# Which tiles lead each block's products, and which queue carries the weight sums, in a hybrid mLSTM, attention and conv-FFN layer

## The chip, the cores and the metric

The kernel runs on one core of a Trainium2 chip. The metric is the device time of one execution in microseconds; less is better. Five engines work side by side, each in the order of its own instruction stream: TensorE (PE, with its weight loads as PEld), VectorE (DVE), ScalarE (ACT), GpSimd (POOL) and SyncE (SP). SP, POOL and others can issue DMA transfers, and a transfer is issued when its engine comes to it and its semaphores allow it.

## The reference

One layer on a prompt of 2048 tokens and on 8 sample streams of 16 tokens (128 rows), all fp32, with D = 1024:

```python
qm, km, vm, om, ip, fp, qa, ka, va = split_in(x @ w_in)     # 4 x 512, 2 x 4, 512, 128, 128 columns
...
hm, C1, n1, m1 = mlstm_chunkwise(qm, km, vm, logi, logf, C0, n0, m0, mchunk)   # 4 heads x 128, chunks of 64
hm = (og * head_norm(hm, g_mlstm_norm)).reshape(B, T, M_WIDTH)
qa, ka = rope(qa, pos), rope(ka, pos)                       # 8 query heads, 2 key heads x 64
ha = swa_prompt(qa, ka, va, attn_sinks)                     # window of own chunk + 2, one learned sink a head
mix = jnp.concatenate([hm, ha], axis=-1) @ w_out
h = layer_norm(DEEPNORM_ALPHA * x + mix, ln1_g, ln1_b)
u = h @ w_up                                                # 1024 -> 5632
c = b_conv + sum(ext[:, j:j + T] * w_conv[j] for j in range(3))     # causal, over tokens
a, g = jnp.split(c, 2, axis=-1)
f = (jax.nn.silu(g) * a) @ w_down                           # 2816 -> 1024
y = layer_norm(DEEPNORM_ALPHA * h + f, ln2_g, ln2_b)
```

The outputs are y for both inputs and the states: C, n, m of the mLSTM, the last keys and values, and the last rows of u.

## The kernel before

Every fp32 operand of a large product is split into two parts, `hi` (a cast to the matmul's format on ACT, L217) and `lo` (the rest, a subtraction on DVE, L218); a product is three matmuls (hi x hi, hi x lo, lo x hi). The large products also use a scheme of seven block products in place of eight, which needs sums and differences of quarters of the weights and of the inputs.

The program has three stages: I, the input projection (0 to some 630 us), O, the output projection with the first normalization (to some 885 us), and F, the conv-FFN, up (to some 1840 us) and down (to the end).

**Stage I.** The 17 tiles of 128 tokens go in four blocks of four (`IBLOCKS`; the sample tile, index 4, goes with block 0). The input of a block comes as four quads of 512 KB, `xr1` to `xr4` (two halves of the tokens by two halves of the features); `x_load` issues their loads on SP's queue, `x_steps` makes the sums (t1 to t4) and the splits (numbers, and "b12"). The columns of w_in other than gates, keys and values go in five groups g, each as seven products s = 1 to 7 (`i_product`, L704; with the sample's own matmuls, L714, in block 0); `i_after` takes their results out of PSUM (L771 and L777 among them). The 264 columns of gates, attention keys and values are not in the scheme: they are "direct tiles" (`i_direct`, L730), one for each tile of tokens, 24 matmuls each (8 steps of the features by 3); `i_keys` takes the result out (L738, L739), turns the keys and stores them. Their weights are units ("g", e, u), loaded as 264 KB pieces (`next_raw`) and split (`next_split`) through a ring that they share with the products' weights (512 KB a piece).

`i_begin` writes PE's order as the list `items`: ("p", b, g, s) for a product and ("t", b, i, e) for a direct tile whose weights are load number e. In block 0, tiles 2 and 3 come first, then the products with the sample tile among them. Each block but the last ends with its tiles 0 and 1 and the next block's tiles 2 and 3; the last block ends with its tiles 0 and 1.

`i_dense` walks `items`. It is woven with the chains of the blocks that are ready (mLSTM and attention, tile by tile: L1070 to L1350), by a planner's costs: each yields a number of nanoseconds for its PE work. During direct tiles of blocks after the first, `chains.hold` is set. So PE's order is written out; for DVE, ACT, POOL and SP the framework's list scheduler sets the order of instructions when the program is built, and it may place work well ahead of where it is written.

**The weight sums.** The down projection's weights also need sums. `d_sums(k, step)` does one of 11 of them in three steps: step 0 takes two buffers (`txy`, the tags of xr1 and xr3, which are free of inputs by then) and loads two 512 KB rows of w_down (L844, L845), step 1 and 2 do two DVE subtractions each (L850 to L853, 128x512), and step 2 stores both to DRAM (`zt`, L855, L856). Eight of the sums stand in stage I, four in its third and four in its fourth block, three in stage O. All loads and stores are on SP's queue.

**The attention's sinks.** For each tile and key head, POOL copies the sinks into the last columns of the score buffer (`sc`, L1297), ahead of the score matmuls.

**Names that come up below.** L1077 to L1080 (`m_rows`) put a row of the mLSTM's running maxima through DRAM (`zM`, two buffers in turn) on POOL's queue; L1150 to L1159 (`m_norm`) is the head norm: statistics `bst` on DVE, then `mr` on ACT and DVE.

## Time and profile before

| | before |
|---|---|
| three runs | 2312.8, 2321.06 (median), 2321.19 us |
| profiled execution | 2316.15 us, its span 2314.3 us |
| mean granted clock of TensorE | 0.996 |
| PE busy | 2281.9 us (99%) |
| PEld busy | 2094.9 us (91%) |
| DVE busy | 1808.1 us (78%) |
| ACT busy | 1269.0 us (55%) |
| POOL busy | 279.5 us (12%) |
| DMA | 632 MB, mean 273 GB/s |

The span runs from the first to the last instruction of the profiled execution; the rest of its time lies around it. In rows of instructions, `out<-in` gives the program's names, and the bracket at the end of a timeline row is the time that the engine sat idle before it and what ended it. A matmul's own duration includes its way through the array, and the matmuls overlap, so that counts per window give the rate better than single durations. The granted clock is 1.00 at full speed.

### The profile page before, as it was taken

How to read it: one execution, taken by the hardware profiler on the slowest of the kernel's cores; microseconds unless marked ns; L12 is line 12 of the kernel's file. 1: busy time of each engine (PE TensorE's matmuls, PEld its weight loads, DVE VectorE, ACT ScalarE, POOL GpSimd, SP SyncE). 2: the span in 40 equal slices, each digit the busy share in tenths (PEclk: the TensorE clock that was granted, in tenths of full speed). 3: DMA queues.
4: the chain of work that ended last, by engine and by line, in shares of the span. 5: the costliest groups of instructions: out<-in, count | busy, mean ns of one | idle time of the engine just before them, and what ended most of it. 6: DMA issues, size and time to landing. Idle time of an engine off the chain costs nothing.

```text
span 2314.3 us, 39788 instructions
## 1 busy us (share of the span) xinstructions
PE 2281.9 (99%) x14293; PEld 2094.9 (91%) x14293; DVE 1808.1 (78%) x3075; ACT 1269.0 (55%) x2377; POOL 279.5 (12%) x509
## 2 busy tenths in 40 slices
PE   8999999999999999999999999999999999999998
PEld 8999989989877778999999999999999978888876
DVE  8777687787688888998788777678766786895987
ACT  5453466776766655555656555555555544444442
POOL 0001000000011212121002000013111200100200
PEclk9999999999999999999999999999999999999999
DMA  7888999999977757888778889978898776756743
GB/s 276 287 308 297 301 309 336 314 310 342 315 269 240 240 201 270 303 319 311 276 289 274 306 304 311 315 264 287 312 294 261 225 282 208 261 175 215 255 157 108
DMA packets 300166, 632.38 MB, mean 273 GB/s; under 512 B 47869, under 2 KB 141121, under 8 KB 299969
## 3 DMA queue, kind: packets, MB, share of 16 engines
q1 hardware_dynamic: 295296, 616.14, 77.9%
q0 software_dynamic: 3520, 10.56, 1.4%
q10 hardware_dynamic: 1152, 3.15, 0.4%
q8 instruction: 113, 1.85, 0.3%
q14 instruction: 85, 0.69, 0.1%
HBM read 458.11 MB, written 171.64 MB: 272 GB/s over the span
## 4 chain that ended last, share of the span: by engine, by line
PE 76%; DVE 5%; DMA 4%; issue 2%; ACT 1%; SPq 0%; POOL 0%; DVEq 0%; ACTq 0%; POOLq 0%
PE dps L1873 19%; PE fup L1873 19%; PE dps L704 7%; PE dps L2083 6%; PE fht L2083 6%; PE fup L2083 6%; PE dps L222 2%; PE dps L224 2%; PE dps L223 2%; PE ppo L1348 1%; PE psc L1303 1%; PE ppt L1342 1%; DVE w L218 1%; PE fht L1697 1%; DMA txy<-wdn 0%
## 5 line engine op out<-in xcount | busy, mean ns | idle before, releaser
L1873 PE MATMUL dps<-hh,uw 128*128 128x384 f32 (+1 forms) x1848 | 478.7, 328 | 2.0 <-DVE u L1904 2.0
L1873 PE MATMUL fup<-hh,uw 128*128 128x384 f32 (+1 forms) x1848 | 478.2, 328 | 1.5 <-ACT ua L1894 1.5
L1873 PEld LDWEIGHTS dps<-hh,uw 128*128 128x128 f32 x1848 | 330.5, 188 | 2.2 <-DVE u L1904 2.2
L1873 PEld LDWEIGHTS fup<-hh,uw 128*128 128x128 f32 x1848 | 330.0, 188 | 2.0 <-ACT ua L1894 1.9
L1930 DVE SCALAR_TENSOR_TENSOR cc<-u,cw,cc 128x768 f32<-128x768 f32 (+1 forms) x264 | 258.1, 978 | 64.9 <-ACT cc L1928 55.5
L1873 PE MATMUL fup<-hl,uw 128*128 128x384 f32 (+1 forms) x924 | 302.5, 327 | 1.7 <-DVE hl L218 1.7
L1873 PE MATMUL dps<-hl,uw 128*128 128x384 f32 (+1 forms) x924 | 302.8, 328 | 0.0
L704 PE MATMUL dps<-w,oh 128*128 128x256 f32 x1344 | 254.3, 284 | 0.7 <-DVE zev L777 0.7
L217 ACT CAST uw<-wraw 128x1024 fp32r<-128x1024 f32 x126 | 123.0, 979 | 223.8 <-PE dps L2083 120.1
L218 DVE TENSOR_TENSOR w<-wraw,w 128x1024 fp32r<-128x1024 f32 (+2 forms) x167 | 189.4, 1141 | 56.1 <-ACT w L217 48.9
L217 ACT CAST w<-wraw 128x1024 fp32r<-128x1024 f32 (+2 forms) x167 | 163.0, 985 | 107.3 <-PE dps L704 38.9
L704 PEld LDWEIGHTS dps<-w,oh 128*128 128x128 f32 x1344 | 210.5, 188 | 11.8 <-issue 8.1
L218 DVE TENSOR_TENSOR uw<-wraw,uw 128x1024 fp32r<-128x1024 f32 x126 | 142.4, 1131 | 65.7 <-ACT uw L217 65.5
L704 PE MATMUL dps<-w,ol 128*128 128x256 f32 x672 | 187.8, 279 | 0.0
L704 PE MATMUL dps<-oh,w 128*128 128x256 f32 x896 | 170.9, 285 | 6.6 <-ACT mr L1153 3.8
L1873 PEld LDWEIGHTS fup<-hl,uw 128*128 128x128 f32 x924 | 173.5, 188 | 2.4 <-DVE hl L218 2.3
L2083 PE MATMUL fup<-uw,fu 128*128 128x512 f32 x726 | 174.2, 396 | 0.6 <-DVE uw L218 0.6
L1873 PEld LDWEIGHTS dps<-hl,uw 128*128 128x128 f32 x924 | 173.8, 188 | 0.0
L2083 PEld LDWEIGHTS fup<-uw,fu 128*128 128x128 f32 x726 | 136.6, 188 | 34.1 <-DVE uw L218 1.1
L2083 PE MATMUL dps<-uw,fu 128*128 128x512 f32 x660 | 165.3, 396 | 1.1 <-DVE uw L218 1.1
L1928 ACT ACTIVATE cc<-u,cw 128x768 f32<-128x768 f32 (+1 forms) x132 | 132.2, 1002 | 57.8 <-DVE u L1910 28.5
L704 PEld LDWEIGHTS dps<-oh,w 128*128 128x128 f32 x896 | 142.2, 191 | 13.1 <-ACT mr L1153 4.1
(318 smaller groups left out, 4567.0 us busy)
## 6 DMA issues: line engine op xcount, KB each, us to landing
uw<-zw SPq DMA_DIRECT2D x176, 512.0 KB, 5.1
zw<-uw SPq DMA_DIRECT2D x88, 512.0 KB, 3.7
w<-zws SPq DMA_DIRECT2D x72, 512.0 KB, 6.2
wv<-wup SPq DMA_DIRECT2D x66, 512.0 KB, 5.0
wraw<-wi SPq DMA_DIRECT2D x65, 512.0 KB, 5.1
wraw<-zt SPq DMA_DIRECT2D x60, 512.0 KB, 4.3
wraw<-wdn SPq DMA_DIRECT2D x45, 512.0 KB, 4.3
wraw<-wo SPq DMA_DIRECT2D x40, 512.0 KB, 4.5
```

What stands on the lines that cost most here:

```text
L217: nc.scalar.copy(hi, src)
L218: nc.vector.tensor_sub(lo, src, hi.bitcast(F32))
L222: mm(out, ah, bh, start=start, stop=False)
L223: mm(out, ah, bl, start=False, stop=False)
L224: mm(out, al, bh, start=False, stop=stop)
L704: mm(o, l, r, start=s in (1, 7) and c == k == i == 0, stop=k == 3 and i == 2, skip_group_check=True)
L1303: nc.tensor.matmul(ps[kvh][:, j, :nk], q[rs, j0 + j], k[rs, sel], start=i == 0, stop=i == 2)
L1342: nc.tensor.transpose(pp[:, j * P:(j + 1) * P], scs[j // 2][:, 2 * kvh + j % 2, kt * P:(kt + 1) * P], self.ident)
L1873: mm(ps, l[:, k], r[:, k], start=s in (1, 7) and k == 0 and i == 0, stop=k == 3 and i == 2, skip_group_check=True)
L1928: S.activation(c[:, v], u[:, 2:2 + n], AF.Identity, bias=w[3], scale=w[2])
L1930: V.scalar_tensor_tensor(c[:, v], u[:, i:i + n], w[i], c[:, v], op0=ALU.mult, op1=ALU.add)
L2083: mm(ps, l[:, k, c], r[:, k], start=s in (1, 4, 7) and u == 0 and k == 0 and i == 0, stop=u == nu - 1 and k == n - 1 and i == 2, skip_grou ...
```

## The change

- *Which tiles lead.* Block 0 now begins with all of tiles 0 to 3. Tiles 0 and 1 are worked together by halves of the features: the first half of both, then the second half of both (`i_direct` takes `halves`). Every later block's four direct tiles stand at the end of the block before, so that the last block ends with products. The gates' weights are thereby loaded and split four times instead of five.
- *Inputs.* In block 0, quad 1 is loaded first, in two transfers, and split in four pieces (before: quad 2, in one transfer, in four pieces); the order of the other loads and splits follows the tiles. In later blocks quads 1 and 2's splits move into the last group of the block before (`passages`), the loads go in the order 1, 3, 2, 4, and the rope tables of tile 0 are loaded together with those of tile 2.
- *Weight sums.* Consecutive sums take the tags of xr1 and xr3, and of xr2 and xr4, in turn. The loads are written earlier: at the first product of the block for its first sum, and at the product s = 4 of the group before for the others. All 44 transfers go through GpSimd's queue.
- *Sinks.* The copy goes from POOL to ACT and stands behind the score maxima on DVE.

The counts of instructions in the programs: PE's matmuls are the same; SP 1471 to 1424, POOL 483 to 508, ACT 2120 to 2150, DVE 3026 to 3018.

```diff
--- before.py
+++ after.py
@@ -340,7 +340,7 @@
         nb = len(IBLOCKS)
         for b in range(nb):
             if b == 0:
-                it += [("t", 0, i, -1) for i in (2, 3)]
+                it += [("t", 0, i, -1) for i in (1, 2, 3)]
 
                 it += [("p", 0, 0, 1), ("t", 0, 4, -1), ("p", 0, 0, 2), ("p", 0, 1, 1), ("p", 0, 0, 7), ("p", 0, 0, 6)]
             else:
@@ -359,9 +359,8 @@
                     it += [("p", b, g, 5), ("p", b, g + 1, 1), ("p", b, g, 3), ("p", b, g, 4)]
                 else:
                     it += [("p", b, g, s) for s in (6, 7, 5, 2, 3, 4)]
-            it += [("t", b, i, b) for i in (0, 1)]
             if b + 1 < nb:
-                it += [("t", b + 1, i, b) for i in (2, 3)]
+                it += [("t", b + 1, i, b) for i in range(4)]
         self.items = it
 
         uq = []
@@ -534,7 +533,11 @@
     def x_load(self, b, *qs):
         for q in qs:
             self.xr[b, q] = r = self.x_raw(q)
-            self.nc.sync.dma_start(r, self.a["xq"][b][(q - 1) // 2, (q - 1) % 2])
+            x = self.a["xq"][b][(q - 1) // 2, (q - 1) % 2]
+            n = 2 if (b, q) == (0, 1) else 1
+            for i in range(n):
+                k = slice(i * 4 // n, (i + 1) * 4 // n)
+                self.nc.sync.dma_start(r[:, k], x[:, k])
 
     def x_steps(self, b, *steps):
 
@@ -559,7 +562,7 @@
                 x = self.xt[0] if s in (7, 6) else r({1: 1, 2: 3, 3: 4, "b12": 2, 5: 2, 4: 4}[s])
 
                 self.hx[b, s] = h, l = self.x_slot(4 if s == "b12" else s)
-                n = 4 if (b, s) == (0, "b12") else 1
+                n = 4 if (b, s) == (0, 1) else 1
                 for i in range(n):
                     k = slice(i * 4 // n, (i + 1) * 4 // n)
                     nc.scalar.copy(h[:, k], x[:, k])
@@ -590,33 +593,35 @@
         last = NG - 1
 
         self.next_raw()
-        self.x_load(0, 2)
-        for _ in range(3):
+        self.x_load(0, 1)
+        self.next_raw()
+        self.x_load(0, 3)
+        for _ in range(2):
             self.next_raw()
-        self.x_load(0, 4)
+        self.x_load(0, 2, 4)
         self.single_raw = self.tp.tile([P, KD, P], F32, name="xsr", tag="pth", bufs=2)
         nc.sync.dma_start(self.single_raw, a["xs"])
         self.angles = {}
-        self.rope_load(IBLOCKS[0][2], 2)
+        for i in (0, 2):
+            self.rope_load(IBLOCKS[0][i], 2)
         self.rope_load(NPT, 1)
         self.next_split()
-        self.x_steps(0, "b12")
-        for _ in range(3):
+        self.x_steps(0, 1)
+        self.next_split()
+        self.x_steps(0, 2)
+        for _ in range(2):
             self.next_split()
-        self.x_steps(0, 3)
+        self.x_steps(0, "b12", 3)
         self.x_single(1, 2)
-        self.x_load(0, 1)
         self.next_raw()
-        self.x_load(0, 3)
-        self.x_steps(0, 1)
         self.advance()
-        self.x_steps(0, 2, "t3", 7, "t2", 6)
+        self.x_steps(0, "t3", 7, "t2", 6)
         self.x_single(4)
         self.x_steps(0, "t1", 5, "t4")
         self.sb, self.trans = {}, None
 
-        passages = [{1: ["load"], 7: ["t3", 7], 6: ["t2", 6], 3: [3, "t4"], 4: ["b12", "t1"]},
-                    {1: ["load"], 6: ["t3"], 7: [7, "t2"], 5: [6], 3: [3, "t4"], 4: ["b12", "t1"]}]
+        passages = [{1: ["load"], 7: ["t3", 7], 6: ["t2", 6], 2: [1], 5: [2], 3: [3, "t4"], 4: ["b12", "t1"]},
+                    {1: ["load"], 6: ["t3"], 7: [7, "t2"], 5: [6], 2: [1, 2], 3: [3, "t4"], 4: ["b12", "t1"]}]
         sums = 0
         after = None
         for item in self.items:
@@ -635,16 +640,18 @@
                     self.advance()
                 if b not in self.gates:
                     self.gates[b] = self.tp.tile([P, 5, 8], F32, name="gates", tag="gates", bufs=2)
+                if b == 0 and ti == 1:
+                    for h in range(2):
+                        for i in range(2):
+                            yield from self.i_direct(b, i, e, self.ib[i * 2], (h,))
+                    self.i_keys(b, 0, self.ib[0])
+                    self.i_keys(b, 1, self.ib[2])
+                    self.advance()
+                    continue
                 ps = self.bank([P, 512], "pg") if ti == 4 else self.ib[ti % 2 * 2]
                 yield from self.i_direct(b, ti, e, ps)
                 self.i_keys(b, ti, ps)
-                if ti == 1:
-                    if b + 1 < nb:
-                        self.x_steps(b + 1, 1, 2)
-                    else:
-                        self.release(4)
-                    after = [6, b + 1]
-                elif ti == 3 and b or ti == 4:
+                if ti == 3 and b or ti == 4:
                     self.release(4)
                     self.x_steps(b, 4)
                     if b:
@@ -663,15 +670,16 @@
                 behind = self.i_after(b, g, s)
             if (b, g, s) == (0, 0, 7):
                 self.t_setup()
-            if (g, s) == (1, 6):
-                self.rope_load(IBLOCKS[b][0], 2)
+            if (g, s) == (last, 4):
+                after = [8, b + 1]
             if g == last and b + 1 < nb:
                 if s == 7:
-                    self.rope_load(IBLOCKS[b + 1][2], 2)
+                    for i in (0, 2):
+                        self.rope_load(IBLOCKS[b + 1][i], 2)
                 for x in passages[b > 0].get(s, ()):
                     if x == "load":
                         self.spare = True
-                        self.x_load(b + 1, 1, 2, 3, 4)
+                        self.x_load(b + 1, 1, 3, 2, 4)
                     else:
                         self.x_steps(b + 1, x)
             if g == last and b + 1 == nb and s in (7, 5, 2, 3):
@@ -679,12 +687,13 @@
             with self.tc.issue_after(behind) if behind and b == 0 else nullcontext():
                 self.advance()
 
-            if b >= nb // 2 and g < last:
-
-                steps = (6, 2, 5) if g == last - 1 else (6, 5, 3)
-                if s in steps:
-                    self.d_sums(sums, steps.index(s))
-                    sums += s == steps[2]
+            if b >= nb // 2:
+
+                if (g, s) == (0, 1) or s == 4 and g < last - 1:
+                    self.d_sums(sums, 0)
+                    sums += 1
+                elif g < last and s in ((2, 5) if g == last - 1 else (5, 3)):
+                    self.d_sums(sums - 1, 2 if s == 3 or g == last - 1 and s == 5 else 1)
         self.sums = sums
         self.logs_of(nb - 1)
         self.chains.hold = False
@@ -715,10 +724,10 @@
                 if k % 2:
                     yield 645
 
-    def i_direct(self, b, ti, e, ps):
+    def i_direct(self, b, ti, e, ps, halves=(0, 1)):
 
         mm = self.nc.tensor.matmul
-        for k in range(KD):
+        for k in [4 * h + i for h in halves for i in range(4)]:
             wh, wl = [w[:, k % 2] for w in self.wu["g", e, k // 2]]
             if ti == 4:
                 xh, xl = [self.hs[1 if k < 4 else 2][:, i, k % 4] for i in range(2)]
@@ -840,9 +849,9 @@
     def d_sums(self, k, step):
         nc, V = self.nc, self.nc.vector
         if step == 0:
-            self.txy = x, y = [self.xp.tile([P, D], F32, name="txy", tag=f"xr{q}", bufs=1) for q in (1, 3)]
-            nc.sync.dma_start(x, self.a["wdn"][k])
-            nc.sync.dma_start(y, self.a["wdn"][NK2 + k])
+            self.txy = x, y = [self.xp.tile([P, D], F32, name="txy", tag=f"xr{q}", bufs=1) for q in ((1, 3), (2, 4))[k % 2]]
+            nc.gpsimd.dma_start(x, self.a["wdn"][k])
+            nc.gpsimd.dma_start(y, self.a["wdn"][NK2 + k])
             return
         x, y = self.txy
         if step == 1:
@@ -852,8 +861,8 @@
             V.tensor_sub(y[:, r], y[:, r], x[:, l])
             V.tensor_sub(y[:, l], y[:, l], y[:, r])
             return
-        nc.sync.dma_start(self.zt[0, k], x)
-        nc.sync.dma_start(self.zt[1, k], y)
+        nc.gpsimd.dma_start(self.zt[0, k], x)
+        nc.gpsimd.dma_start(self.zt[1, k], y)
 
     def rope(self, A, t, nt):
 
@@ -1294,7 +1303,6 @@
             sc = self.work("sc", [P, 4, 2 * P + 4], bufs=2)
             mx, sm = [self.work(n, [P, 4], bufs=2) for n in ("amx", "asm")]
             w = lambda x: x.rearrange("p (k j) -> p k j", k=2)
-            nc.gpsimd.tensor_copy(sc[:, :, N:N + 1].rearrange("p (k j) o -> p k (j o)", k=2), sink)
             ps = [self.bank([P, 2, 2, P], "psc") for _ in range(2)]
             for j in range(2):
                 for i, (q, k) in enumerate(((qh, self.kh), (qh, self.kl), (ql, self.kh))):
@@ -1308,6 +1316,7 @@
                                            op0=ALU.add, op1=ALU.max, accum_out=mx[:, c:c + 1])
 
             V.scalar_tensor_tensor(w(mx), w(mx), -0.125, nsink, op0=ALU.mult, op1=ALU.min)
+            nc.scalar.copy(sc[:, :, N:N + 1].rearrange("p (k j) o -> p k (j o)", k=2), sink)
             return sc, mx, sm
 
         def exps(sc, mx, sm):
```

## The prediction

> **What bounds the kernel now.** I read the page's busy shares first, then busy time by windows over the stages, then what PE waits for, and at the few places where PE sits idle the timeline and the chain of waits.
>
> ```profile
> span 2314.3 us, 39788 instructions
> ...
> PE 2281.9 (99%) x14293; PEld 2094.9 (91%) x14293; DVE 1808.1 (78%) x3075; ACT 1269.0 (55%) x2377; POOL 279.5 (12%) x509
> ```
>
> TensorE (PE) is the bound: 2314.3 - 2281.9 = 32.4 us idle. The change leaves the number of matmuls as it is (the changed program's order on each engine shows the same 14293), so it can only win idle time and time at a low clock, or lose some. Each row of the next view is a window (us from the start), its length, the busy time of PE, PEld, DVE, ACT and POOL with instruction counts, PE's granted clock, DMA share and GB/s.
>
> ```profile
> 0.00:45.00 45.00, 37.34 (x241) 34.17 (x242) 38.54 (x65) 24.51 (x39) 0.31 (x5) 0.92 0.75 272
> 45.00:250.00 205.00, 204.27 (x1767) 199.78 (x1766) 151.32 (x237) 91.84 (x143) 10.80 (x9) 1.00 0.87 300
> ...
> 300.00:345.00 45.00, 40.37 (x329) 37.58 (x329) 36.92 (x113) 30.49 (x80) 2.94 (x6) 0.96 0.95 311
> ...
> 440.00:640.00 200.00, 197.77 (x1629) 181.09 (x1629) 152.81 (x440) 144.43 (x366) 15.83 (x32) 1.00 0.94 315
> ```
>
> Three windows carry what this change can touch: the start (7.7 us idle), 300 to 345, in the third block of the input projection (4.6 us), and the fourth block (2.2 us). The quiet stretch gives the price of a matmul in the stream: 204.27 / 1767 = 0.116 us. The direct tiles are 264 columns wide instead of 256, so I estimate 0.119 us for theirs, 24 x 0.119 = 2.9 us a tile.
>
> ```profile
> 8.97:12.39 3.42, 1.81 (x13) 1.40 (x12) 2.89 (x4) 2.15 (x3) 0.00 (x0) 1.00 1.04 406
> 12.39:15.80 3.41, 3.41 (x18) 3.41 (x17) 3.04 (x8) 2.78 (x8) 0.00 (x0) 0.50 1.03 420
> 36.28:39.70 3.42, 1.82 (x14) 1.43 (x12) 3.42 (x6) 2.78 (x3) 0.00 (x0) 1.00 0.97 388
> 39.70:43.11 3.41, 3.41 (x19) 3.41 (x18) 3.14 (x5) 1.11 (x2) 0.00 (x0) 0.50 0.70 246
> 326.41:329.83 3.42, 0.05 (x1) 0.00 (x0) 3.27 (x15) 1.20 (x3) 0.00 (x0) 1.00 0.77 215
> 329.83:333.24 3.41, 2.94 (x13) 2.94 (x14) 3.41 (x9) 2.27 (x6) 0.00 (x0) 0.50 1.11 344
> ```
>
> These are pairs. After a stretch of 3.4 us in which PE was busy for 1.8 us or less, the next 3.41 us ran at a granted clock of 0.50. Half of 3.41 is 1.7 us lost, each time, on top of the gaps themselves. PE looks fully busy there, so the idle sum hides it.
>
> The middle one hangs on the weight sums. The rows are, in order, PE's longest wait, two steps of the chain of waits, DVE and ACT rows of the timeline, and the chain's end.
>
> ```profile
> PE dps L704 <- ACT mr L1153: 3.8, 1, 3.8
> ...
> 317.33 0.32 SPq L856
> ...
> 317.74 7.43 DMA txy<-wdn
> ...
> 325.20 0.69 DVE L850 TENSOR_TENSOR txy<-txy 128x512 f32<-128x512 f32 x1 [3.92 <-DMA txy<-wdn]
> 325.81 0.29 DVE L1150 BATCH_NORM_STATS2 bst<-pnum 128x6 f32<-128x128 f32 x1
> ...
> 328.63 0.17 ACT L1153 ACTIVATE mr<-pnum 128x2 f32<-128x2 f32 x1 [3.17 <-DVE bst L1150]
> ...
> 329.66 0.59 ACT L771 ACTIVATE zev<-dps 128x512 f32<-128x512 f32 x1
> ...
> 330.32 4.75 PE dps L704 x27
> ```
>
> The second sum's load could start only when the first sum's store had been issued (one buffer pair); it took 7.43 us; DVE, in order, sat 3.92 us on it with the mLSTM's statistics (bst) queued behind; ACT waited 3.17 us for those, and the copy (L771) that frees the PSUM bank stood behind that on ACT. PE idled 3.8 us and then ran 3.4 us at half clock: 3.8 + 1.7 = 5.5 us.
>
> **The start.**
>
> ```profile
> 4.58 0.41 ACT L565 CAST oh<-xr 128x256 fp32r<-128x256 f32 x1 [2.56 <-DMA xr<-xq]
> ...
> 5.93 0.39 PE L730 MATMUL dps<-w,oh 128*128 128x264 f32 x1
> ...
> 10.03 0.51 PE L730 MATMUL dps<-w,oh 128*128 128x264 f32 x2 [0.86 <-ACT oh L565]
> ...
> 11.29 0.39 PE L730 MATMUL dps<-w,ol 128*128 128x264 f32 x1 [0.75 <-DVE ol L566]
> ...
> 17.06 0.28 PE L704 MATMUL dps<-oh,w 128*128 128x256 f32 x1
> ```
>
> Before, two direct tiles (48 matmuls, 5.7 us of work) fill 5.93 to 17.06, 11.1 us: 5.4 us are lost in waits for the second half of the input quad and of the splits, 1.7 of it in the half-clock window. After, four tiles (96 matmuls, 11.4 us) lead, the first two by halves of the features, so that 24 matmuls need only the first half quad and the first two weight pieces, and the next ones use each later piece twice. At 406 GB/s (the 8.97 window) 256 KB arrive in 0.65 us and 512 KB in 1.3 us. Counted from the 4.58 row (there a whole 512 KB quad had landed), the first half quad is there at 3.9, the gate pieces and the second half by 5.9, the next quad at 7.2, the last gate pieces at 7.9 and 8.6, quad 2 at 9.9, quad 4 at 11.2. PE starts where it does now and needs a new piece only every 1.4 to 2.9 us; I leave it 1.4 us of waits (about the two 0.8 us waits shown). First product at 5.93 + 11.4 + 1.4 = 18.7, with 5.7 us more work done: a gain of 17.06 + 5.7 - 18.7 = 4.1 us.
>
> ```profile
> 28.17 1.22 DVE L218 TENSOR_TENSOR w<-wraw,w 128x1024 fp32r<-128x1024 f32 x1
> ...
> 34.47 0.51 PE L704 MATMUL dps<-oh,w 128*128 128x256 f32 x2 [0.48 <-DVE w L218]
> 38.02 0.38 PE L704 MATMUL dps<-oh,w 128*128 128x256 f32 x1 [0.76 <-ACT w L217]
> 39.35 0.53 PE L704 MATMUL dps<-oh,w 128*128 128x256 f32 x2 [0.84 <-DVE w L218]
> 44.43 0.39 PE L704 MATMUL dps<-oh,w 128*128 128x256 f32 x1 [0.69 <-ACT zev L771]
> ```
>
> From 17 to 45 us DVE's splits (1.22 us for each 512 KB) run just behind PE. The 5.7 us more of direct work ahead of the products need only 128x528 gate pieces and no full weight unit, so DVE gets that much lead and the four waits (0.48 + 0.76 + 0.84 + 0.69 = 2.8 us) and the second half-clock window (1.7) can go. The input splits are pulled ahead of the products too, so I give back 1.5 us: 3.0 us gained. Together -7.1 us (bounds -9 for all of it, and 0 if DVE stays the bound).
>
> The Trainium skill's "TensorE: Matmul & The Clock Gate" (Part 1, and "HAM oscillation") has half rate only after an idle window of about 3.4 us. The trace differs: before 12.39 and 39.70 PE was busy for half of the window, with waits of at most 0.86 us, and it was halved all the same. By the page's rule 3.4 us of the 7.1 would stay lost, since they would not come from these gaps.
>
> **Block ends.** Later blocks get all four direct tiles of the next block at the end of the one before, instead of two of their own and two of the next: the same matmuls, with 16 instead of 20 gate loads and four fewer gate splits on ACT and DVE, which hide behind PE: 0. The last block now ends without its 48 direct matmuls (5.7 us), which covered the wait for the last chain steps; by the last 200 us window, idle for only 2.2 us in all, little waits there, and products of the output projection are at hand: +0.6 (0 to +3).
>
> **The weight sums.** 44 transfers move from SP's queue to GpSimd's, and consecutive sums alternate between two buffer pairs.
>
> ```profile
> wraw<-wg SPq DMA_DIRECT2D x20, 264.0 KB, 4.1
> ...
> zt<-txy SPq DMA_DIRECT2D x22, 512.0 KB, 5.2
> ...
> txy<-wdn SPq DMA_DIRECT2D x22, 512.0 KB, 5.2
> ...
> y<-yacc POOLq DMA_DIRECT2D x12, 512.0 KB, 4.8
> ...
> wi<-zM POOLq DMA_DIRECT2D x16, 258.0 KB, 5.0
> ...
> DMA to landing us min/median/max: 3.3/5.2/9.8
> ...
> L1080 POOL DMA_DIRECT2D wi<-zM x16 | 9.2, 575 | 63.6 <-DMA zM<-r_M 58.6 <-DMA wraw<-wi 5.0
> ```
>
> From issue to landing a 512 KB transfer on GpSimd's queue takes 4.8 us here, as on SP's (5.2, from 3.3 to 9.8). An issue costs GpSimd 0.58 us, 44 x 0.58 = 25 us of an engine that is 12% busy. But GpSimd's queue is in order too: a load stands behind wi<-zM, which waited 58.6 us in all, over its 16, for zM<-r_M to land, and behind the earlier sum's store, which waits for DVE.
>
> The Trainium skill ("SBUF — State Buffer", the "DVE blocks DMA" trap) speaks against GpSimd's queue: 620 ns alone become some 3100 beside a DVE two-port copy. The two POOLq rows above, taken with DVE 78% busy, show no such loss; by the page each load would land some 2.5 us later, an estimate.
>
> In the third block the order decides. In the changed order all four sums of the block stand within about 85 DVE instructions (before: about 210), directly ahead of the same bst. Two pairs serve four sums, so the third and fourth load again wait for a store. With the first pair free at about 317 as now, its loads issue at 318 to 320 and land 5 to 7 us later, at 323 to 327; four DVE subtractions of 0.69 us share that time, and bst comes at 325.1 to 328.6 instead of 325.8. The stall stays where it is: +1.2 us (-0.7 to +3).
>
> ```profile
> 516.33 0.69 DVE L851 TENSOR_TENSOR txy<-txy 128x512 f32<-128x512 f32 x1 [4.37 <-DMA txy<-wdn]
> ```
>
> In the fourth block this DVE wait of 4.37 us goes, and by the same estimate of landings up to three of 2 to 6 us come 20 to 45 us earlier, where the changed order has the loads wait for a store; part is hidden by PE's own lead: +0.7 (-1.2, about half of the idle 2.2, to +3).
>
> **Sink copies.**
>
> ```profile
> L1297 POOL COPY sc<-k_sink 128x4 f32<-128x4 f32 x32 | 10.2, 322 | 46.6 <-PE ppt L1342 39.2 <-PE ppt L1518 3.8 <-PE ppo L1528 3.3
> ```
>
> 32 copies of 128x4 leave POOL for ACT, whose nearest row is the 128x2 one above at 0.17 us: 32 x 0.17 = 5.4 us on an engine 45% idle, off the path: 0 (bounds: 0 to +1 where one delays a bank copy). The rest of the kernel, from the last block of the output projection on, keeps its order on every engine: 0.
>
> **Sum.** -7.1 + 1.2 + 0.7 + 0.6 = -4.6. The profiled execution took 2316.15 us (span 2314.3); that is 4.9 below the median of the three runs, 2321.06, and inside their 2312.8 to 2321.2. So 2316.15 - 4.6 = 2311.6, or 2312. From no change, 0.5% (11.6 us) is what a measurement of this kernel can tell.
>
> **The rivals.** *The sums stop stalling (A).* If the earlier issue carries the loads clear of their use, 5.5 us in the third block and about 1.2 in the fourth go as well: -7.1 - 6.7 + 0.6 = -13.2, 2303. For it: the loads are written up to two products earlier and have a second pair. Against it: four sums packed before one bst. 0.18.
>
> *GpSimd's loads land too late (B), the other side.* DVE takes the subtractions in order, so each late load holds bst, ACT's bank copy and PE, at the 5.5 us of the one event. Eight sums lie in the third and fourth block. Four further such events cost 22 us: -7.1 + 22 + 0.6 = +15.5, 2332. It decides from the fourth event on (three are +10, within 0.5%). For it: DVE's waits of 3.92 and 4.37, the in-order queue behind wi<-zM. Against it: of the before waits on txy only one reached PE at such a price. 0.15.
>
> *The start is DVE's (C).* The splits of inputs and units have the same total, and PE only waits later: 0 instead of -7.1, 2318.6. For it: DVE is busy 38.5 of the first 45 us. 0.12.
>
> *Half clock stays (D).* The two windows come again at other places of the start, 3.4 us: 2315. This is where the page's rule would lead. 0.10.
>
> **How the numbers follow.** The forecast has 0.45. Forecast, C and D are within 0.5%: 0.67; A is faster, 0.18; B slower, 0.15. The range reaches 2300 (A with a little more at the start) and 2328 (B with three events, or the upper bounds of the sums on C: 2316.2 + 3 + 3 + 3 + 1 = 2326); beyond it lie the heavier part of B and the edge of A, under 0.2.
>
> **What would show it.** Right: the first window with PE idle for some 4 us fewer and no 0.50 clock between 12 and 43; the first L704 product near 18.7; PE's wait for mr near 326 still there with DVE's wait for txy before it, and a txy landing from POOLq near 5 us. Wrong: more 0.50 windows in 300 to 640 (B), none (A), or waits of PE on DVE's splits between 19 and 45 as before (C).

## Result and the profile after

The changed kernel took 2330.82 us (median of six runs, 2329.62 to 2333.03) against 2319.01 us for the kernel before (six runs, 2312.8 to 2321.19). The ratio is 1.0058, with a 95% interval from 1.0042 to 1.0075: 0.6% slower, where a faster kernel was forecast, and above the range of 2300 to 2328 us.

Two lines of the changed kernel's profile page, then the row of GpSimd's drains in the changed kernel (L2191) and in the kernel before (L2182). From here on a line number is that of the kernel whose trace is shown.

```profile
span 2331.1 us, 39740 instructions
...
PE 2285.4 (98%) x14293; PEld 2097.2 (90%) x14293; DVE 1807.9 (78%) x3071; ACT 1270.6 (55%) x2405; POOL 282.7 (12%) x521
```

```profile
L2191 POOLq DRAIN  x3: 40/102/8221, 2322.1 to 2330.8; - x3
```

```profile
L2182 POOLq DRAIN  x3: 45/93/4627, 2308.8 to 2314.0; - x3
```

The two drain rows give shortest, median and longest duration in ns. At the end of the program GpSimd's sequencer drains its queue: 4.63 us before, 8.22 us after. In both kernels this drain starts some 2.5 us ahead of the end of DVE's last instruction (at 2308.8 and 2322.1 us), and in the changed kernel only a few semaphore steps follow it. From DVE's last instruction to the end of the span the kernel before takes 2.9 us and the changed one 6.5, so 3.5 us of the loss come behind the last arithmetic.

The rest is in the input projection. The same stretches as were shown of before, and then five pairs of windows of 3.41 us and a sixth pair at 336 us. Columns are as before: start and end, length, busy time of PE, PEld, DVE, ACT and POOL, granted clock, DMA share, GB/s.

```profile
0.00:45.00 45.00, 38.15 (x285) 35.94 (x285) 38.70 (x72) 25.24 (x43) 0.31 (x5) 1.00 0.75 269
45.00:250.00 205.00, 200.87 (x1719) 196.01 (x1720) 150.66 (x244) 89.40 (x134) 10.80 (x9) 0.99 0.86 294
300.00:345.00 45.00, 38.47 (x311) 36.85 (x311) 35.53 (x94) 24.66 (x65) 8.44 (x17) 0.96 1.02 367
440.00:640.00 200.00, 193.44 (x1593) 179.22 (x1591) 144.42 (x402) 139.03 (x356) 22.51 (x38) 0.98 0.92 310
```

```profile
148.23:151.64 3.41, 1.56 (x13) 1.35 (x12) 1.39 (x3) 1.57 (x3) 0.31 (x1) 1.00 0.75 268
151.64:155.05 3.41, 3.41 (x18) 3.41 (x18) 1.72 (x3) 0.71 (x2) 0.00 (x0) 0.51 0.77 219
325.78:329.19 3.41, 0.80 (x7) 0.64 (x7) 3.41 (x8) 0.99 (x4) 1.68 (x4) 1.00 0.92 224
329.19:332.60 3.41, 3.41 (x17) 3.41 (x18) 0.99 (x7) 0.00 (x0) 0.00 (x0) 0.50 0.88 303
346.26:349.67 3.41, 1.31 (x9) 0.73 (x7) 1.75 (x3) 2.08 (x6) 2.13 (x3) 1.00 0.97 337
349.67:353.08 3.41, 3.41 (x15) 3.06 (x15) 2.02 (x3) 3.41 (x10) 0.00 (x0) 0.50 1.04 405
510.10:513.51 3.41, 1.01 (x8) 1.01 (x9) 0.49 (x3) 3.09 (x9) 0.99 (x2) 1.00 0.88 305
513.51:516.92 3.41, 3.41 (x18) 3.41 (x17) 2.80 (x6) 1.35 (x3) 1.08 (x2) 0.50 0.98 374
520.34:523.75 3.41, 1.53 (x14) 1.36 (x13) 3.38 (x7) 3.41 (x13) 0.47 (x1) 1.00 0.97 282
523.75:527.17 3.42, 3.42 (x18) 3.42 (x17) 3.39 (x7) 3.42 (x7) 0.54 (x1) 0.50 1.02 412
...
336.02:339.43 3.41, 1.80 (x16) 1.60 (x15) 2.11 (x4) 1.00 (x3) 1.70 (x4) 1.00 1.01 297
339.43:342.84 3.41, 2.65 (x23) 2.65 (x24) 3.41 (x16) 1.79 (x7) 0.00 (x0) 1.00 1.00 405
```

The first window gained: 285 matmul records in 45 us instead of 241, and no 0.50 clock there. But 45 to 250 is no longer quiet, and in the third and fourth block there are four windows at half clock instead of one. The pair at 336 us did not lose its clock, although PE was busy for only 1.80 us in its first window; the wait of 2.37 us there runs on into the second. PE's rows, read at the same point of the work (in the first five rows 5.7 us are taken off the changed kernel's time for the two more direct tiles that it has done there; the woven chains may still differ a little at a point), say where:

| point | before, us | after, us | after less before, same work |
|---|---|---|---|
| end of block 0's product 3 of group 0 | 56.1 | 58.3 | -3.5 |
| end of block 0's products | 155.2 | 160.1 | -0.8 |
| end of block 1's products | 289.9 | 296.3 | +0.7 |
| block 2, start of product 6 of group 1 | 339.2 | 351.5 | +6.6 |
| block 3, start of product 1 of group 0 | 467.0 | 480.2 | +7.5 |
| end of the input projection's matmuls | 629.0 | 642.7 | +13.7 |
| end of DVE's last instruction | 2311.3 | 2324.6 | +13.3 |
| span | 2314.3 | 2331.1 | +16.8 |

The profiled execution before is 2.9 us below its median and the one after 2.1 us above, which is why +16.8 stands beside +11.8 for the medians.

### The profile page after: what moved, and what is told of

Read it like the earlier page. It is cut to its first block, busy times and chain, and to the rows that moved or that the text cites. A ratio compares the mean times of both kernels' runs of the same rounds, so it can differ in the third digit from the quotient of the medians.

```text
span 2331.1 us, 39740 instructions
## 1 busy us (share of the span) xinstructions
PE 2285.4 (98%) x14293; PEld 2097.2 (90%) x14293; DVE 1807.9 (78%) x3071; ACT 1270.6 (55%) x2405; POOL 282.7 (12%) x521
## 3 DMA queue, kind: packets, MB, share of 16 engines
q8 instruction: 113, 1.85, 0.3%
```

## Experiments

All ratios are against the kernel before, run on the same chip. The code cuts show the lines that matter, with `...` for what is left out.

| what | median, us | ratio, 95% interval |
|---|---|---|
| sums as before | 2316.71 | 1.0006 (0.9995 to 1.0018) |
| sums alone | 2334.97 | 1.0085 (1.0070 to 1.0099) |
| sums on SP | 2320.52 | 1.0020 (1.0011 to 1.0030) |
| start alone | 2319.85 | 1.0012 (1.0000 to 1.0024) |
| stores on SP | 2330.35 | 1.0057 (1.0044 to 1.0069) |
| loads on SP | 2319.70 | 1.0009 (0.9999 to 1.0019) |
| gates first | 2313.63 | 0.9986 (0.9974 to 0.9997) |
| queue alone | 2347.90 | 1.0133 (1.0118 to 1.0148) |
| sums later on DVE | 2328.64 | 1.0055 (1.0042 to 1.0068) |
| two pairs, held back, SP | 2318.65 | 1.0008 (0.9997 to 1.0020) |
| one pair, held back, SP | 2314.58 | 0.9992 (0.9983 to 1.0001) |
| GpSimd's waits only | 2316.28 | 0.9991 (0.9981 to 1.0001) |
| held back in the last block | 2311.81 | 0.9975 (0.9966 to 0.9984) |
| GpSimd's queue, gates first | 2322.83 | 1.0023 (1.0011 to 1.0035) |
| loads behind ms | 2320.93 | 1.0010 (0.9995 to 1.0025) |
| sinks on GpSimd | 2313.99 | 0.9981 (0.9970 to 0.9992) |

**Sums as before** (the changed kernel with the old `d_sums`):

```diff
-for q in ((1, 3), (2, 4))[k % 2]]
+for q in (1, 3)]
-nc.gpsimd.dma_start(...)        # four of them; the calls at their old places
+nc.sync.dma_start(...)
```

> The changed kernel with the weight sums as they were: one buffer pair, SP's queue, the old places. Theory S (the sums are the loss: in the changed kernel DVE waits 14.5 + 5.9 us for txy and PE idles 2 to 3 us at 326, 337, 505, 510 and 521 us): it is faster than the kernel before by about 1 us at 160 us (start gain 3.7, less 2.8 for the new wait near 149 us), and ends within 4 us of it, 2313 to 2319 us; the five waits named are gone. Rival T (the tiles' new order is the loss, since it packs the chains' work behind the block's start): it stays near the changed kernel, 2326 to 2331 us.

2316.71 us, ratio 1.0006. The sums are the loss (1.0058 less 1.0006, some 12 us), and the tiles bring nothing that can be measured. PE's wait at 149 us was there as in the changed kernel.

**Sums alone** (the kernel before with the changed `d_sums` and its calls).

> The kernel before with only the sums changed: two pairs, earlier places, GpSimd's queue. Theory S: slower than before by 10 to 16 us, 2328 to 2335 us, with DVE's waits for txy near 15 to 20 us in all, and POOL's last drain longer than the 4.6 us of before by some 3 us. Rival T: within 4 us of before.

2334.97 us: the loss is there without the tiles, at the upper end of what was expected. DVE waited 13.5 + 6.0 us for txy, and the last drain took 8.22 us.

**Sums on SP** (the changed kernel, `nc.sync.dma_start` for all four transfers of a sum).

> The changed kernel with the sums' 44 transfers on SP's queue instead of GpSimd's; two pairs and the new places stay. Theory Q (the queue is what delays the loads: y of the third sum was issued at 326.1 us, behind wi<-zM which waited for zM to land at 324.8): the loads are issued up to 5 us earlier, DVE's waits for txy fall from 20 us to under 8 and the time falls by 6 to 12 us, to 2319 to 2325 us; the last drain of POOL is back at 4.6 us. Rival P (packing all sums ahead of one set of head norm statistics is what costs, whatever the queue): the time falls by the drain alone, 2 to 4 us.

2320.52 us, 10 us less than the changed kernel, and the drain is 4.63 us again. But DVE's waits for txy fell only from 20 to 17 us. The queue costs, and not by DVE's waits alone. What the second pair and the new places cost by themselves would be the 0.14% over the sums as before (1.0020 and 1.0006), but the two intervals overlap.

**Start alone** (the kernel before with block 0's items, loads and splits of the changed kernel; block 0's end still has tiles 2 and 3 of block 1).

> The kernel before with only block 0's start changed: tiles 0 to 3 lead, 0 and 1 by halves, the inputs loaded in the new order. Later block ends, sums and sink copies as before. The changed kernel was 3.7 us ahead at 58 us for the same work, so 3.7 us faster than before if nothing takes it back (2313 to 2317 us); if the wait near 149 us belongs to the start and not to the block's end, only 1 us faster, 2316 to 2320 us.

2319.85 us, ratio 1.0012. Its trace has the start's gain and then PE idle 2.5 us at 149 and 2.4 us at 161: the waits belong to the start's new order, and take the gain back. At 329 us PE also waited longer than before, 5.7 us in place of 3.8.

**Stores on SP**, then **loads on SP** (the other two transfers stay on GpSimd's queue).

> The changed kernel with the sums' loads on GpSimd's queue and their stores on SP's. Theory O (order: on GpSimd's queue a load stands behind the stores, which wait for DVE, and behind wi<-zM): with the stores gone from it, half of the late loads go and the time falls by 3 to 8 us, to 2322 to 2327 us. Rival G (a transfer on GpSimd's queue is itself slower): it stays, 2328 to 2333 us, and txy's median landing is over 6 us as with both on it. Both theories: the last drain of POOL, 4.63 us with 28 transfers on its queue and 8.22 with 72, is 6.4 us with 50.

> The changed kernel with the sums' loads on SP's queue and only their stores on GpSimd's. Theory O: the loads no longer stand behind wi<-zM, but still wait for the stores to land; close to both on SP (2320.5), plus the longer drain (6.4 us in place of 4.63): 2320 to 2324 us. Rival G: half way between both on SP and both on GpSimd's queue, 2325 to 2327 us.

2330.35 and 2319.70 us. The stores on GpSimd's queue cost nothing that these runs resolve, their part of the drain included (2319.70, and 2320.52 with all on SP's); the loads on it cost all of the 10 us. Of theory O the half on the stores fell. The last drain is 6.42 us in both, as expected:

```profile
L2191 POOLq DRAIN  x3: 40/93/6422, 2323.6 to 2330.5; - x3
```

Counted in the traces, 44, 66 and 88 transfers on GpSimd's queue gave 4.63, 6.42 and 8.22 us, 0.082 us for each one added. (The expectation's 28 left out the 16 zM<-r_M.) Landing hardly differed: the loads took a median of 6.1 us from issue on GpSimd's queue, and 5.8 with all on SP's. The Trainium skill's "SBUF — State Buffer" (the "DVE blocks DMA" trap) has such transfers wait for descriptors that GpSimd cannot write beside some DVE copies; the landing times show no loss of the 2.5 us estimated from it. The other queue, which the page advises, was the faster one for the loads all the same.

**Gates first** (sums as before, and the later gate loads at high priority in the scheduler):

```diff
-            nc.sync.dma_start(e[0], a["wg"][u[2]])
+            with self.tc.high_priority() if u[1] >= 0 else nullcontext():
+                nc.sync.dma_start(e[0], a["wg"][u[2]])
```

> The changed tiles and sink copies with the sums as before, and the later gate weight loads given priority on SP's queue. With the sums as before PE waited 2.2 us at 149 us for a bank copy on ACT that stood behind a split of the second gate piece, whose load was issued at some 146 us; half clock followed (1.7 us). If the late load is the cause, the wait and the half-clock window go: 3 to 4 us faster than with the sums as before (2316.7), about 2313 us. Rival: ACT's or DVE's own load (two more input splits in that group) is the cause, and it stays near 2316 us with a wait at the same place.

2313.63 us, and the wait at 149 us is gone. The intervals of the two versions still overlap a little (up to 0.9997, and from 0.9995), so the gain rests on the trace as well. In the changed kernel ACT's and SP's rows there read:

```profile
145.86 1.05 ACT L568 CAST oh<-wraw 128x1024 fp32r<-128x1024 f32 x1
150.07 0.63 ACT L217 CAST w<-wraw 128x528 fp32r<-128x528 f32 x1 [3.16 <-DMA wraw<-wg]
150.60 0.58 ACT L780 COPY zev<-dps 128x512 f32<-128x512 f32 x1
```

```profile
140.88 0.46 SPq L457 DMA_DIRECT2D wraw<-wg  x1
...
144.37 1.73 SPq L762 DMA_DIRECT2D zv<-zev  x2
146.15 0.91 SPq L457 DMA_DIRECT2D wraw<-wg  x2
```

The second gate piece was issued at 146.15 behind stores that wait for ACT; its split stood ahead of the copy that frees the PSUM bank; PE got the bank 1.85 us late and then ran 3.4 us at half clock. In the kernel before, the first two loads had gone at 136.5 and 141.2. With priority they go at 139.7 and 143.4.

**Queue alone** (the kernel before, the four transfers on GpSimd's queue, one pair, old places).

> The kernel before with only the queue changed: the sums' 44 transfers on GpSimd's queue, one buffer pair and the old places. The longer drain alone is +3.5 us (2319.7 against 2316.2). Theory O: one pair makes each load stand behind the store before it anyway, so late loads add 0 to 5 us: 2320 to 2325 us. Rival P (the packing by two pairs and earlier places is what makes the queue hurt): the drain alone, 2319 to 2321 us; the two differ where DVE's waits for txy are over the 11.0 us of before.

2347.90 us, over 20 us more than either theory allowed. DVE waited 29.0 + 9.0 us for txy. GpSimd waited 22.3 + 7.6 us in front of loads for an earlier sum's store to land. The second pair and earlier places of the change are a remedy for its queue (1.0133 to 1.0085 without the tiles), not part of the harm.

**Sums later on DVE** (the changed kernel, all on GpSimd's queue, with the subtractions not placed on DVE ahead of the last emitted weight split):

```diff
+        with self.tc.issue_after(self.last_split) if step else nullcontext():
+            ...                     # the subtractions and stores
```

> The changed kernel, all 44 transfers still on GpSimd's queue, with one thing added: the sums' subtractions may not be placed on DVE ahead of the weight split that was emitted last when they are written. In DVE's order the eight sums then stand at instructions 445 to 991, spread over the blocks, instead of 378 to 463 and 736 to 821, and the head norm's statistics are no longer behind them. Theory V (what costs is DVE's place for the subtractions, ahead of their data, because the scheduler takes a load on GpSimd's queue for early): DVE's waits for txy in the third and fourth block go to near 0, and the time is that with the sums as before (2316.7) plus the 3.5 us of the drain: 2319 to 2322 us. Rival O2 (the loads' late issue on GpSimd's queue and their traffic cost by themselves): it stays above 2326 us.

2328.64 us with no DVE wait for txy at all. Theory V fell: late data on DVE is not the whole cost; the wait at 149 us is still in this version. Its trace has new waits instead: PE 2.88 us at 369, where ACT waited 5.5 us for the head norm's `ms` on GpSimd, and 3.1 us at 441, where the next block's inputs came late. Those are loaded into the sums' buffers, and the stores that free them stood on GpSimd's queue behind wi<-zM:

```profile
425.84 0.58 POOL L1093 DMA_DIRECT2D wi<-zM  x1 [4.24 <-DMA zM<-r_M]
426.41 0.53 POOL L868 DMA_DIRECT2D zt<-txy  x1
427.18 0.53 POOL L869 DMA_DIRECT2D zt<-txy  x1 [0.24 <-DVE txy L866]
```

**Two pairs** and **one pair, held back, on SP** (both with gates first).

> All mended: the changed tiles and sink copies, two pairs, the sums' transfers on SP's queue, their subtractions held back on DVE as above, and the gate loads first. Theory V: faster than with the sums as before and the gates first (2313.6), since no txy wait is left: 2307 to 2312 us. Rival: the second pair only adds what DVE had slack for, 2313 to 2316 us.

> As the last, with one buffer pair and the sums' loads at their old places. With the subtractions held back, a second pair is worth nothing if loads land in time with one: within 2 us of the two-pair version. If one pair's load after the store is still too late, 3 to 5 us slower than it, with DVE's waits for txy over 5 us.

2318.65 and 2314.58 us. Both expectations fell: two pairs are no better than one, and slower by 4 us, with no wait for txy in either. With two pairs PE waits 1.9 and 0.8 us at 435 us for weights kept in DRAM (w<-zws), with one 1.3 and 0.7; why two pairs cost the rest was not found.

**GpSimd's waits only** (two pairs held back, with the lines added) and **held back in the last block** (one pair held back, with the condition narrowed to three of the fourth block's sums):

```diff
+            for t in (x, y):
+                nc.gpsimd.memset(t[:, :1], 0.0)
             nc.sync.dma_start(x, self.a["wdn"][k])
```

```diff
-        with self.tc.issue_after(self.last_split) if step else nullcontext():
+        with self.tc.issue_after(self.last_split) if step and k in (4, 5, 6) else nullcontext():
```

> The version with two pairs, SP's queue, subtractions held back and gates first (2318.65), with one thing added: before each sum's loads GpSimd writes one column of each of the two buffers (128x1), so that GpSimd waits for the buffer as it would with the load on its own queue, while all transfers stay on SP's. Theory H (a load that waits for its buffer holds up GpSimd's own work behind it: the norm's ms, zM and wi; ACT's waits for ms then delay a bank copy): slower by 3 to 8 us, 2321 to 2327 us, with an ACT wait for ms over 4.5 us and a PE wait after it in 340 to 640 us. Rival Q (it is the transfers on GpSimd's queue, not GpSimd's waiting): within 2 us of 2318.65. The last drain of POOL stays 4.63 us in both.

> The best so far (changed tiles, sums as before, gates first, 2313.6), with the subtractions of three of the fourth block's four sums held back on DVE. With them held back everywhere PE lost 0.7 us in 500 to 560 us instead of 7.9, but lost more from 400 to 440 and from 580 to 640. Expected: the first gain without the loss from 400 to 440: 2309 to 2312 us. Rival: what is held back comes back from 580 to 640 us, and it stays within 2 us of 2313.6.

2316.28 us: theory H as it was put fell. GpSimd waited 35.6 us for stores to land ahead of these writes, and nothing came of it. But in its order the writes stood behind the norm's ms and not in front of it (ACT never waited over 3.4 us for ms). The second, with one pair on SP's queue, is the best version: 2311.81 us, ratio 0.9975, 0.25% faster than before.

**GpSimd's queue, gates first** (the sums later on DVE, plus the gates' priority, and a priority for the head norm's ms on GpSimd as well) and **loads behind ms** (the same without that priority for ms, with the loads held behind the last ms emitted on GpSimd: `issue_after(self.last_split if step else self.last_ms)`).

> All transfers of the sums on GpSimd's queue, two pairs, subtractions held back on DVE (2328.64), with the gate loads first. GpSimd's order is unchanged around the sums: at 364 us of that trace two loads that wait for their buffers stand ahead of the head norm's ms, and ACT waits 5.5 us for ms. If the parts add up: 2328.6 less the 2.4 us wait and 1.7 us half clock at 149 us, 2324 to 2327 us, with the wait for ms and PE's 2.9 us at 369 us still there.

> The same as the last, with the sums' loads held behind the last ms emitted on GpSimd, so that none that waits stands ahead of the next ms; all transfers stay on GpSimd's queue. Theory H (what waits in GpSimd's order holds up the norm): 3 to 5 us faster than the last, 2320 to 2322 us, with no ACT wait for ms over 4 us and no PE wait at 369 us. Rival (the queue's transfers themselves, or its stores behind wi<-zM, which delay the next block's inputs): within 2 us of the last.

GpSimd's rows of the first and then of the second, at the same tile:

```profile
362.49 0.53 POOL L858 DMA_DIRECT2D txy<-wdn  x1 [4.11 <-DMA zt<-txy]
365.36 0.54 POOL L859 DMA_DIRECT2D txy<-wdn  x1 [2.33 <-DMA zt<-txy]
365.91 1.05 POOL L1175 TENSOR_TENSOR ms<-mr,mhalf 128x4 f32<-128x4 f32 x1
```

```profile
362.05 1.04 POOL L1174 TENSOR_TENSOR ms<-mr,mhalf 128x4 f32<-128x4 f32 x1 [3.08 <-DVE mr L1173]
363.06 0.59 POOL L858 DMA_DIRECT2D txy<-wdn  x1
```

In the first, two loads wait for their buffers in front of ms, which is 3.9 us later than in the second; ACT and PE follow:

```profile
366.99 0.40 ACT L1181 ACTIVATE hn<-hn,ms 128x128 f32<-128x128 f32 x1 [4.46 <-POOL ms L1175]
367.30 0.58 ACT L809 COPY dps<-dps 128x512 f32<-128x512 f32 x1
```

```profile
367.93 0.39 PE L714 MATMUL dps<-w,oh 128*128 128x256 f32 x1 [1.87 <-ACT dps L809]
```

The second has neither wait: a load that waits on GpSimd's queue holds up GpSimd's arithmetic, and that reached PE. The totals, 2322.83 us (under the 2324 to 2327 expected) and 2320.93, do not decide between theory H and its rival: they lie 1.9 us apart and their intervals overlap, so the size of this alone is not measured.

**Sinks on GpSimd** (the best version, with the sink copies as before).

> The best so far (2311.8) with the 32 sink copies back on GpSimd. Off the path in both theories: within 1 us of 2311.8. If the copies on ACT delay bank copies, up to 3 us faster.

2313.99 us against 2311.81, with overlapping intervals: no difference that these runs resolve.

## Why the prediction was wrong

- *The start, -7.1.* Right in sign, half in size: -3.5, which is little more than the 3.4 us of the two half-clock windows. These did go in this execution; with the same start, the version with the sums on SP's queue had one at 52 us, so it is in part luck. The waits did not shrink. The first product came at 20.4 us, not at 18.7: the direct tiles began at 5.5 and lost 3.5 us, not 1.4, most of it in waits for weight splits. So the term of 4.1 was 2.4. The term of 3.0 was 1.1: the lead did not free DVE, and PE still waited for it afterwards, 1.37 us at once. The rule of the Trainium skill ("TensorE: Matmul & The Clock Gate", Part 1), by which half clock comes after an idle window of some 3.4 us, does not fit the five half-clock windows after either: PE had been busy 0.80 to 1.56 us in the windows before them, and its longest single wait there is 2.61 us.

```profile
11.64 0.39 PE L739 MATMUL dps<-w,oh 128*128 128x264 f32 x1 [0.89 <-DVE w L218]
...
20.39 0.28 PE L713 MATMUL dps<-oh,w 128*128 128x256 f32 x1
...
33.48 0.51 PE L713 MATMUL dps<-oh,w 128*128 128x256 f32 x2 [1.37 <-DVE w L218]
```

- *Block ends, 0.* Wrong. The gate splits were counted, but not where their loads stand in SP's order. Moved behind two waiting stores, one of them took back 2.7 us by 160 us. Gates first removed it (1.0006 to 0.9986).
- *The third block, +1.2.* This is the step that failed, together with the next one, and lost the sign: +5.9 (from +0.7 to +6.6). The sum timed the third sum's loads and let bst come right behind their landing, at 325.1 to 328.6. It named the fourth sum's load, which waits for a store, but gave it no time, and it named wi<-zM ahead of the loads and put nothing of that in the sum. GpSimd's queue shows the loads waiting, the last one 7.25 us:

```profile
325.33 0.55 POOL L1089 DMA_DIRECT2D wi<-zM  x1 [2.64 <-DMA zM<-r_M]
326.12 0.53 POOL L854 DMA_DIRECT2D txy<-wdn  x1 [0.24 <-DMA zt<-txy]
326.64 0.54 POOL L865 DMA_DIRECT2D zt<-txy  x1
328.31 0.53 POOL L853 DMA_DIRECT2D txy<-wdn  x1 [1.14 <-DMA zt<-txy]
336.09 0.53 POOL L854 DMA_DIRECT2D txy<-wdn  x1 [7.25 <-DMA zt<-txy]
```

  DVE, ACT and PE, in order of time:

```profile
324.67 0.69 DVE L859 TENSOR_TENSOR txy<-txy 128x512 f32<-128x512 f32 x1 [1.01 <-DMA txy<-wdn]
328.28 0.68 DVE L1141 TENSOR_TENSOR dt<-pscore,dt 128x512 f32<-128x512 f32 x1
329.06 1.96 PE L1220 MATMUL pnum<-v,dt 128*128 128x129 f32 x8 [2.61 <-issue]
332.22 0.69 DVE L860 TENSOR_TENSOR txy<-txy 128x512 f32<-128x512 f32 x1 [2.42 <-DMA txy<-wdn]
337.32 0.69 DVE L859 TENSOR_TENSOR txy<-txy 128x512 f32<-128x512 f32 x1 [2.96 <-DMA txy<-wdn]
337.93 0.49 DVE L1159 BATCH_NORM_STATS2 bst<-pnum 128x6 f32<-128x128 f32 x2
338.51 0.17 ACT L1162 ACTIVATE mr<-pnum 128x2 f32<-128x2 f32 x1 [2.41 <-DVE bst L1159]
340.19 0.39 PE L713 MATMUL dps<-oh,w 128*128 128x256 f32 x1 [2.37 <-ACT zev L780]
```

  Thirteen of the block's sixteen subtractions stood ahead of bst, the last of them the fourth sum's first. bst came at 337.93, which is 332.2 with the 5.7 us taken off. The path that the prediction named (bst, mr, the bank copy, PE) cost PE 2.37 us at 338 us. At 326 us, where the prediction had it, PE waited 2.61 us for something else: dt, which stood on DVE behind nine subtractions and was done 0.1 us before PE went on. From 347 us it waited 1.17, 0.44 and 0.48 us for the head norm's `hn`. Two windows ran at half clock.
- *The fourth block and the end of the stage, +0.7 and +0.6.* +6.2 together. The prediction had up to three waits of 2 to 6 us on DVE, part of them hidden by PE's lead. DVE waited 7.22 and 3.49 us, with the mLSTM's `col` behind the first, and little was hidden: PE was idle 2.2, 2.4 and 1.9 us near 507, 512 and 523 us, and two windows ran at half clock, for which the term had nothing:

```profile
506.64 0.69 DVE L859 TENSOR_TENSOR txy<-txy 128x512 f32<-128x512 f32 x1 [7.22 <-DMA txy<-wdn]
507.25 0.18 DVE L1035 COPY col<-pcol 128x36 f32<-128x36 f32 x1
507.49 0.39 PE L1311 MATMUL psc<-kringh,qh 64*128 64x256 f32 x2 [2.23 <-DVE col L1035]
512.50 0.39 PE L713 MATMUL dps<-oh,w 128*128 128x256 f32 x1 [2.45 <-ACT zev L780]
514.08 0.69 DVE L860 TENSOR_TENSOR txy<-txy 128x512 f32<-128x512 f32 x1 [3.49 <-DMA txy<-wdn]
523.14 0.46 PE L1220 MATMUL pnum<-v,dt 128*128 128x129 f32 x2 [1.88 <-DVE asm L1327]
```

  In both blocks the prediction took GpSimd's queue for equal to SP's because a transfer takes as long on it. With the loads alone moved back to SP's queue the loss is all but gone (2319.70 us, ratio 1.0009).
- *Issue on GpSimd, 0.* The issues are hidden, but the drain of its queue at the end is not: +3.5 us, a term that the sum does not have.
- *The rivals.* B had the sign, and late loads were its reason. Its price was 5.5 us an event, where 326 us cost 2.61 + 1.7 = 4.3 and 523 us 1.88 + 1.7 = 3.6; the changed kernel has four half-clock windows in the two blocks and before one, so three further events, not B's four. Its path, bst and the bank copy, is the one at 338 us alone; at 326 and 507 us other work of the chains stood behind the subtractions on DVE. That its +10 for three events lies near the +11.8 of the medians is luck in part: the start gained only half of what B's sum took for it, and the drain and the wait at 149 us are not in that sum. It was given 0.15, since only one wait on txy had reached PE before.
- *What stays open.* Of the 10 us between the two queues, some 3.5 are the drain. Moving the loads changes two things at once: when they are issued, and the order that the scheduler gives DVE. With the loads on SP's queue and the stores on GpSimd's, four subtractions of the third block stand ahead of that dt, not nine, and eight ahead of bst, not thirteen; PE waited there 0.23 and 1.50 us, and no window of the block ran at half clock. That the sixteen stand close together is not what decides: they are DVE's instructions 378 to 463 in the changed kernel, and 393 to 468 in that fast version. With the subtractions held back and the gates first, GpSimd's queue cost 4.2 us over SP's (2322.83 and 2318.65, the first with the priority for ms too), little more than the drain. So the other 6 or so us came with DVE's order and with what waited behind the loads; how they divide was not separated.

## What to carry to other kernels

Before a transfer is moved to an engine's queue, list what that engine computes behind it and what the transfer waits for there; equal landing times do not make the queues equal. A new order at one place moves loads on a shared queue elsewhere, so look for the loads that the scheduler has put behind waiting stores, and give those priority. Waits cost PE more than themselves when together they leave a 3.41 us window half empty, so add up the idle time of a window: here 1.17 us at a stretch with smaller ones beside it cost a half-clock window, and 2.37 us that fell across the border of two windows did not.

## What the runs showed of the hardware

The program's last drain of GpSimd's queue grows with the transfers issued on it: 4.63, 6.42 and 8.22 us with 44, 66 and 88, that is 0.082 us for each one added. It starts some 2.5 us before the last arithmetic ends, and the rest lies behind it. Half clock for one window of 3.41 us followed windows in which PE was busy for 0.05 to 1.82 us; of the eight shown of the two kernels, only the one at 326 us before holds a single wait of over 3.4 us. Read over all 18 traces, between the first 7 us and the last matmuls, each of the 45 windows at full clock in which PE was busy for at most 1.59 us was followed by one at 0.50. Of the 19 with 1.63 to 1.82 us only four were, and none with more.
